# Sums of weight blocks in a gated recurrence: by VectorE from plain loads, and x's block sums kept out of the weight ring

## The chip, the cores and the metric

The kernel runs on one core of one Trainium2 chip. The metric is the device time of one execution in microseconds (us); of several runs the median is given. TensorE does the matrix products, VectorE and ScalarE the elementwise work, GpSimd (POOL) some products of the recurrence and every accumulating transfer, SyncE (SP) issues the plain loads.

## The reference

The program is a two-layer trunk on x of 512 frames by 1024 channels, all float32. Layer 0 is a gated linear recurrence (8 heads of 128 channels) and a squared-ReLU MLP; then one shared K/V is projected; layer 1 is differential attention over it and a second MLP. The change touches layer 0's mixer alone:

```python
proj = rms_norm(h) @ w_in
q, f, i, g = split(proj)            # queries, forget gates, values, output gates
k, log_f = gates(f)
o = hgrn2_recurrence(silu(q), k, log_f, i)
o = rms_norm(o) * silu(g)           # then @ w_out
```

## The kernel before, in words

Everything is held transposed (channels on partitions). Each float32 operand of a product is split into a rounded part ("hi") and a remainder ("lo"), and TensorE makes three matmuls for one: hi by hi, hi by lo, lo by hi. Weights arrive by SP into a ring of four raw slots (tag `raw`), are split by ScalarE (hi) and VectorE (lo) into rings of eight slots (tags `whi`, `wlo`), and free those when the last matmul that reads them is done. `split_b` (line 194) makes both parts by engines. `split_d` (line 184) lets ScalarE write hi and the negated hi, and an accumulating transfer of POOL's queue adds the weights from memory to the latter; it reads the raw slot only on ScalarE.

The mixer (`hgrn`, line 790) goes over four pairs of heads. For every head it projects q and f (`qf`), and spawns a chain (`head`, line 799) of gating, seven levels of a recursive scan, the state (`st`, lines 872 to 880), the output (`o`, lines 882 to 887) and a norm. The state's later chunks are made by VectorE at line 879, and the `o` products need them. The output gates of pairs 1 to 3 (`gates_pair`, line 902) and the values of pairs 2 and 3 (`values_pairs`, line 956) are made by a seven-product scheme: the weight matrix is cut in four blocks (0: A11, 1: A22, 2: A12, 3: A21), and four sums of blocks are wanted beside the blocks themselves: s1 = 3 + 1, s3 = 3 + 0, s2 = 0 + s1, s4 = 2 + s2. The products come in the order a11, s1, a12, s2, s4, s3, a22. Four sums of x's blocks meet them (`block_sums`, line 694): it runs as a chain, in the tiles `e` and `f` that are taken from the raw ring.

For a gates pair SP loads blocks 0 and 2 into `ra`, block 3 twice into the halves of `rs`, and block 1 into `rd`; POOL's queue then adds blocks 0 and 1 to `rs` by an accumulating transfer (line 910), which gives s3 and s1. VectorE makes s2 and s4 at lines 915 and 916. For the values every sum s1, s3 is likewise a load of block 3 (line 965) and an accumulating transfer on top (line 970).

The order on TensorE is written out by the program itself: `Plan` (line 45) steps through the chains by costs of its own (the `W_` constants) and the yields. On the other engines and queues a scheduler fixes the order when the kernel is built, by priority (chains are put ahead, `CHAIN_AHEAD`) and by its own reckoning of when each instruction could start. Every engine then runs its list in order: an instruction whose input is late holds up all behind it.

```python
            g.dma_start(rs, src[:, 0:2, :], accum_op=ALU.add)                       # 910
            v.tensor_tensor(ra[:, 0, :], ra[:, 0, :], rs[:, 1, :], op=ALU.add)      # 915
                v.scalar_tensor_tensor(st[:, c, :], st[:, c - 1, :], tcur[:, c:c + 1], ps[:, c * P:(c + 1) * P],   # 879
```

Of the kernel before, what the change touches and what calls it, by code (L numbers as in the profile page):

```python
# [9 lines left out]
F32 = mybir.dt.float32  # L10
F32R = mybir.dt.float32r
# [3 lines left out]
ALU = mybir.AluOpType  # L15
AX = mybir.AxisListType

P = 128
D = 1024
S = 512  # L20
# [68 lines left out]
def trunk_kernel(ctx: ExitStack, tc: tile.TileContext, x_t, w_qf, w_g, w_gs, w_i, w_is, w_ao, w_kv, w_q, w_bo, w_up, w_us, w_dn,  # L89
# [33 lines left out]
    xlo = [cp.tile([P, 2, S], F32R, name=f"xlo{i}") for i in range(4)]  # L123
    xraw = [cp.tile([P, 2, S], F32, tag=f"uhi{i}", name=f"xraw{i}", bufs=1) for i in range(4)]
    uhi = [cp.tile([P, 2, S], F32R, tag=f"uhi{i}", name=f"uhi{i}", bufs=1) for i in range(4)]
    ulo = [cp.tile([P, 2, S], F32R, name=f"ulo{i}") for i in range(4)]

    res = [x_t.rearrange("(k p) t -> p k t", p=P)[:, :, lo:hi] for lo, hi in ((0, 256), (256, 512))]
    gn = cp.tile([P, G_N], F32, name="gn")
# [564 lines left out]
    def block_sums(xs, ts):  # L694

        gain = gn[:, G_APRE:G_APRE + 8]
        e, f = [wp.tile([P, 4, 256], F32, tag="raw", name=f"sum_x{i}", bufs=4) for i in range(2)]

        def split(src, sign, n):
            if n < 3:  # L700
                hi, lo = [wp.tile([P, 4, 256], F32R, tag=t, name=f"{t}_x{n}", bufs=8) for t in ("whi", "wlo")]
            else:
                hi, lo = [u[3].rearrange("p j (r t) -> p (j r) t", r=2) for u in (uhi, ulo)]
            a.activation(hi, src, AF.Copy, scale=sign)
            if sign > 0:
                v.tensor_tensor(lo, src, hi.bitcast(F32), op=ALU.subtract)
            else:
                v.scalar_tensor_tensor(lo, src, -1.0, hi.bitcast(F32), op0=ALU.mult, op1=ALU.subtract)
            ts.append([(hi[:, r, :], lo[:, r, :]) for r in range(4)])

        def odd(n, out, op):

            for r in range(4):
                v.scalar_tensor_tensor(out[:, r], xs[2 * r + 1][:, n * 256:n * 256 + 256], gain[:, 2 * r + 1:2 * r + 2],
                                       out[:, r], op0=ALU.mult, op1=op)

        for r in range(4):
            for n, t in enumerate((e, f)):
                a.activation(t[:, r], xs[2 * r][:, n * 256:n * 256 + 256], AF.Copy, scale=gain[:, 2 * r:2 * r + 1])
        v.tensor_tensor(e, e, f, op=ALU.subtract)  # L720
        split(e, 1.0, 0)
        yield 8.0
        odd(1, f, ALU.subtract)
        split(f, 1.0, 1)
        yield 8.0
        odd(1, e, ALU.add)
        split(e, -1.0, 2)
        yield 8.0
        odd(0, e, ALU.subtract)
        split(e, -1.0, 3)  # L730

# [58 lines left out]
    def hgrn(hp, w0, xs):  # L790
# [108 lines left out]
        def banks(name):  # L899
            return [mmt(f"{name}_{n}") for n in "xyz"]  # L900

        def gates_pair(p):

            src, nm = w_gs[p - 1], f"gs{p}"
            ra = wp.tile([P, 2, 512], F32, tag="raw", name=f"raw_a{nm}", bufs=4)
            nc.sync.dma_start(ra, src[:, 0:3:2, :])
            rs = wp.tile([P, 2, 512], F32, tag="raw", name=f"raw_s{nm}", bufs=4)
            for i in range(2):
                nc.sync.dma_start(rs[:, i, :], src[:, 3, :])
            g.dma_start(rs, src[:, 0:2, :], accum_op=ALU.add)  # L910
            rd = wp.tile([P, 1, 512], F32, tag="raw", name=f"raw_d{nm}", bufs=4)
            nc.sync.dma_start(rd, src[:, 1:2, :])
            a11, a12 = split_d(ra, src[:, 0:3:2, :], f"a{nm}")
            s3, s1 = split_b(rs, f"s{nm}")
            v.tensor_tensor(ra[:, 0, :], ra[:, 0, :], rs[:, 1, :], op=ALU.add)
            v.tensor_tensor(ra[:, 1, :], ra[:, 1, :], ra[:, 0, :], op=ALU.add)
            s2, s4 = split_b(ra, f"t{nm}")
            a22, = split_d(rd, src[:, 1:2, :], f"d{nm}")
            x, y, z = [b[:, 0:256] for b in banks(nm)]
            g0, g1 = ggs[2 * p], ggs[2 * p + 1] = [hp.tile([P, S], F32, tag="g", name=f"g_{2 * p + j}", bufs=4) for j in range(2)]  # L920
            lo, hi = slice(0, 256), slice(256, 512)
            t1, t3, t2, t4 = ts

            def prod(ps, w, b, first):
                for k in range(4):
                    mm3(ps, w[0][:, k * P:(k + 1) * P], w[1][:, k * P:(k + 1) * P], *b[k], first and k == 0, k == 3, True)
                    yield 0

            def swish(gg, sign):
                if sign > 0:  # L930
                    v.tensor_tensor(gg, gg, rb, op=ALU.mult)
                else:
                    v.scalar_tensor_tensor(gg, gg, -1.0, rb, op0=ALU.mult, op1=ALU.mult)
                e = hp.tile([P, S], F32, tag="e", name=f"e{nm}{sign}", bufs=1)
                a.activation(e, gg, AF.Sigmoid)
                v.tensor_tensor(gg, gg, e, op=ALU.mult)

            yield from prod(x, a11, xpart(0, 0), True)
            a.activation(g0[:, lo], x, AF.Copy)
            yield from prod(z, s1, t1, True)  # L940
            a.activation(g1[:, hi], z, AF.Copy)
            yield from prod(y, a12, xpart(1, 0), True)
            v.tensor_tensor(g0[:, lo], y, g0[:, lo], op=ALU.add)
            yield from prod(x, s2, t2, False)
            a.activation(g0[:, hi], x, AF.Copy)
            yield from prod(z, s4, xpart(1, 1), False)
            v.tensor_tensor(g0[:, hi], z, g0[:, hi], op=ALU.add)
            swish(g0, 1)
            yield from prod(x, s3, t3, False)
            v.tensor_tensor(g1[:, hi], x, g1[:, hi], op=ALU.add)  # L950
            a.activation(g1[:, lo], x, AF.Copy)
            yield from prod(y, a22, t4, True)
            v.tensor_tensor(g1[:, lo], y, g1[:, lo], op=ALU.add)
            swish(g1, -1)

        def values_pairs():
# [6 lines left out]
            def block(n, i):  # L963
                r = raw(n)
                nc.sync.dma_start(r, w_is[:, i:i + 1, :])
                return r

            def summed(n, i):
                r = block(n, 3)
                g.dma_start(r, w_is[:, i:i + 1, :], accum_op=ALU.add)  # L970
                return r

            ra = block("a", 0)
            a11, = split_d(ra, w_is[:, 0:1, :], f"a11{nm}")
            rs = summed("s1", 1)
            s1, = split_b(rs, f"s1{nm}")
            rb_ = block("b", 2)
            a12, = split_d(rb_, w_is[:, 2:3, :], f"a12{nm}")
            v.tensor_tensor(ra, ra, rs, op=ALU.add)
            s2, = split_b(ra, f"s2{nm}")  # L980
            v.tensor_tensor(rb_, rb_, ra, op=ALU.add)
            s4, = split_b(rb_, f"s4{nm}")
            s3, = split_b(summed("s3", 0), f"s3{nm}")
            a22, = split_d(block("d", 1), w_is[:, 1:2, :], f"a22{nm}")
            x, y, z = [b.rearrange("p (m f) -> p m f", m=2) for b in banks(nm)]
            v0, v1 = vts[2], vts[3] = [hp.tile([P, 4, 256], F32, tag="vt", name=f"vt{p}", bufs=3) for p in (2, 3)]
            t1, t3, t2, t4 = ts
# [35 lines left out]
        for p in range(4):  # L1023
# [42 lines left out]
            else:  # L1066
# [2 lines left out]
                    yield until(("mix", 2 * p - 4), ("mix", 2 * p - 3))  # L1069
                if p == 2:  # L1070
                    yield from values_pairs()
                yield from gates_pair(p)
            done(("g", p))

    def values(ps, wv, t2):
# [276 lines left out]
```

## Time and profile before

| what | us |
|---|---|
| median of 3 runs | 1283.62 |
| lowest and highest of them | 1283.18, 1285.72 |
| the profiled execution, its own time | 1281.38 |
| its span, first to last instruction | 1279.3 |
| TensorE busy in the span | 1241.0 |
| VectorE, ScalarE, POOL busy | 820.6, 674.1, 100.2 |

The profile is one execution, separate from the three runs; its time lies 2.08 above its span and 2.24 below their median. The recurrence takes the first quarter of the span; TensorE's mean granted clock is 0.991 of full speed. A timeline row of the trace has the start, the duration, engine, line, operation with the tiles written and read, their shapes and the count; in brackets stands how long the engine was idle before it and what ended that. A transfer's row on SP, SPq or POOL is its issue; when it lands is told apart.

### The profile page before, as it was taken

What the parts mean: (1) busy time and instruction counts of PE and PEld (TensorE: products, weight loads), DVE (VectorE), ACT (ScalarE), POOL (GpSimd) and SP (SyncE); (2) the same over time, 40 slices, a digit from 0 to 9 for tenths busy, and PEclk for the clock granted to TensorE, in tenths of its full rate; (3) what the DMA queues carried; (4) which work ended last, traced back from release to release, by engine and by line L of the source; (5) the groups of instructions that cost most, each with busy time, mean ns of one, the idle gap of its engine ahead of it and who ended that gap; (6) DMA issues with size and microseconds to landing.
All of it is one profiled execution on the core that took longest, in us unless ns stands there. A gap on an engine that the chain in (4) does not pass through costs nothing.

```text
span 1279.3 us, 21468 instructions
## 1 busy us (share of the span) xinstructions
PE 1241.0 (97%) x8440; PEld 1125.2 (88%) x8440; DVE 820.6 (64%) x1646; ACT 674.1 (53%) x1248; POOL 100.2 (8%) x171
## 2 busy tenths in 40 slices
PE   9989997999999999999999999999999999999996
PEld 7778897899997988989999887889998898998996
DVE  7857783785863654745659977665785473653646
ACT  7435545435861652734645877665784271561732
POOL 0202211101000000000100000001000000000010
PEclk9999999999999999999999999999999999999999
DMA  7143848342547563564625523314236356363531
GB/s 240 57 101 102 170 108 193 79 137 90 173 130 134 138 176 91 166 148 104 201 73 168 149 66 100 112 38 132 79 122 180 98 168 142 103 194 70 157 108 66
DMA packets 58502, 161.94 MB, mean 127 GB/s; under 512 B 6529, under 2 KB 8834, under 8 KB 58402
## 3 DMA queue, kind: packets, MB, share of 16 engines
q1 hardware_dynamic: 46400, 121.13, 30.1%
q0 software_dynamic: 11760, 39.33, 14.8%
q8 instruction: 66, 1.08, 0.3%
q14 instruction: 34, 0.28, 0.1%
q10 hardware_dynamic: 242, 0.13, 0.1%
HBM read 150.86 MB, written 9.70 MB: 126 GB/s over the span
## 4 chain that ended last, share of the span: by engine, by line
PE 64%; DVE 5%; ACT 4%; DMA 3%; issue 2%; DVEq 0%; ACTq 0%; POOLq 0%; SPq 0%
PE dn L114 21%; PE ux L114 7%; PE up L114 7%; PE kq L114 6%; PE dn_h L114 5%; PE bo_h L114 3%; PE uz L114 3%; PE ao_h L114 3%; DMA raw_s<-in_w_us_dram 3%; PE v L114 2%; PE lg L114 2%; PE uy L114 1%; PE ao L114 1%; DVE wlo_s L200 1%; PE pt L119 1%
## 5 line engine op out<-in xcount | busy, mean ns | idle before, releaser
L114 PE MATMUL dn<-uhi,whi_dn 128*128 128x512 f32 x384 | 152.1, 396 | 0.0
L114 PE MATMUL dn<-ulo,whi_dn 128*128 128x512 f32 x384 | 152.0, 396 | 0.0
L114 PE MATMUL dn<-uhi,wlo_dn 128*128 128x512 f32 x384 | 151.9, 396 | 0.0
L114 PEld LDWEIGHTS dn<-uhi,whi_dn 128*128 128x128 f32 x384 | 72.3, 188 | 17.7 <-ACT r L562 0.7
L114 PEld LDWEIGHTS dn<-uhi,wlo_dn 128*128 128x128 f32 x384 | 72.3, 188 | 17.3
L114 PEld LDWEIGHTS dn<-ulo,whi_dn 128*128 128x128 f32 x384 | 72.3, 188 | 16.8
L199 ACT ACTIVATE whi_a<-raw_a 128x1024 fp32r<-128x1024 f32 x24 | 25.4, 1059 | 116.3 <-PE dn L114 113.1
L172 DVE TENSOR_TENSOR wlo_dn<-raw_dn,whi_dn 128x1024 fp32r<-128x1024 f32 x64 | 76.5, 1219 | 5.3 <-ACT whi_dn L171 4.6
L467 DVE TENSOR_TENSOR ulo<-r,uhi 128x1024 fp32r<-128x1024 f32 (+1 forms) x40 | 40.2, 1010 | 53.2 <-ACT uhi L466 53.1
L114 PE MATMUL up<-xhi,whi_up 128*128 128x256 f32 x256 | 72.1, 282 | 0.0
L114 PE MATMUL up<-xhi,wlo_up 128*128 128x256 f32 x256 | 71.6, 280 | 0.5 <-DVE wlo_up L172 0.5
L114 PE MATMUL up<-xlo,whi_up 128*128 128x256 f32 x256 | 71.4, 279 | 0.0
L171 ACT ACTIVATE whi_dn<-raw_dn 128x1024 fp32r<-128x1024 f32 x64 | 65.7, 1051 | 6.5 <-PE ux L114 2.9
L114 PE MATMUL dn_h<-uhi,whi_dn 128*128 128x256 f32 x240 | 66.7, 278 | 0.0
L114 PE MATMUL dn_h<-uhi,wlo_dn 128*128 128x256 f32 x240 | 66.3, 276 | 0.0
L114 PE MATMUL dn_h<-ulo,whi_dn 128*128 128x256 f32 x240 | 66.3, 276 | 0.0
L609 DVE TENSOR_TENSOR zacc<-dn,zacc 128x512 f32<-128x512 f32 x32 | 22.1, 690 | 59.1 <-PE dn L114 59.0
L511 POOL DMA_DIRECT2D raw_s<-in_w_us_dram x24 | 20.8, 865 | 487.2 <-DMA raw_s<-in_w_us_dram 335.2
L114 PE MATMUL qf<-xhi,whi_qf 128*128 128x512 f32 x128 | 53.0, 414 | 0.8 <-ACT xhi L678 0.8
L114 PE MATMUL qf<-xhi,wlo_qf 128*128 128x512 f32 x128 | 50.7, 396 | 1.4 <-DMA wlo_qf<-in_w_qf_dram 1.4
L199 ACT ACTIVATE whi_t<-raw_a 128x1024 fp32r<-128x1024 f32 x24 | 25.5, 1061 | 49.4 <-PE dn L114 27.2
L114 PE MATMUL qf<-xlo,whi_qf 128*128 128x512 f32 x128 | 50.9, 397 | 0.3 <-DVE xlo L679 0.3
(530 smaller groups left out, 4139.2 us busy)
## 6 DMA issues: line engine op xcount, KB each, us to landing
raw_dn<-in_w_dn_dram SPq DMA_DIRECT2D x64, 512.0 KB, 4.3
raw_a<-in_w_us_dram SPq DMA_DIRECT2D x24, 512.0 KB, 4.2
raw_s<-in_w_us_dram SPq DMA_DIRECT2D x48, 256.0 KB, 4.2
raw_s<-in_w_us_dram POOLq DMA_DIRECT2D x24, 512.0 KB, 6.4
raw_up<-in_w_up_dram SPq DMA_DIRECT2D x16, 512.0 KB, 3.9
raw_wkv<-in_w_kv_dram SPq DMA_DIRECT2D x16, 512.0 KB, 3.8
raw_qf<-in_w_qf_dram SPq DMA_DIRECT2D x14, 512.0 KB, 3.9
raw_d<-in_w_us_dram SPq DMA_DIRECT2D x12, 512.0 KB, 4.4
```

Of the source, the lines that this page charges most:

```text
L114: nc.tensor.matmul(out, lhsT, rhs, **kw)
L119: nc.tensor.transpose(out, in_, identity)
L171: last_split[:] = [a.activation(hi, raw, AF.Copy)]
L172: v.tensor_tensor(lo, raw, hi.bitcast(F32), op=ALU.subtract)
L199: a.activation(hi, raw, AF.Copy)
L200: v.tensor_tensor(lo, raw, hi.bitcast(F32), op=ALU.subtract)
L467: v.tensor_tensor(ulo[pr][:, :, lo:hi], r, uhi[pr][:, :, lo:hi].bitcast(F32), op=ALU.subtract)
L511: g.dma_start(rs, ws[p, :, 0:2, :], accum_op=ALU.add)
L609: v.tensor_tensor(z, pss[n4], z, op=ALU.add)
```

## The change

Three things are edited.

1. `block_sums` takes `e` and `f` from two new tiles that share memory with `ulo[1]` and `ulo[2]` (where the mixer's output goes later), so that the raw ring keeps four slots for weights. Its steps are spaced anew: a pause of 2 after each of the four pairs of ScalarE copies, then 5 in place of 8 between the sums.
2. A gates pair loads blocks 0 and 2 into `ra` and blocks 1 and 3 into `rs`, each once. `split_d` of block 1 comes before the sums; then VectorE adds block 3 to block 1 (s1) and block 0 to block 3 (s3) in place. The accumulating transfer of line 910, the second load of block 3 and the tile `rd` are gone. The weights' part becomes a function of its own, called at the same point.
3. The values load blocks 0, 3, 1, 3 and 2, and VectorE makes s1 and s3; the two accumulating transfers of line 970 are gone. Block 2 is now the fifth of the five tiles that go through the ring of four.

```diff
--- before.py
+++ after.py
@@ -123,7 +123,8 @@
     xlo = [cp.tile([P, 2, S], F32R, name=f"xlo{i}") for i in range(4)]
     xraw = [cp.tile([P, 2, S], F32, tag=f"uhi{i}", name=f"xraw{i}", bufs=1) for i in range(4)]
     uhi = [cp.tile([P, 2, S], F32R, tag=f"uhi{i}", name=f"uhi{i}", bufs=1) for i in range(4)]
-    ulo = [cp.tile([P, 2, S], F32R, name=f"ulo{i}") for i in range(4)]
+    sums = [cp.tile([P, 4, 256], F32, tag=f"ulo{i}", name=f"sums{i}", bufs=1) for i in (1, 2)]
+    ulo = [cp.tile([P, 2, S], F32R, tag=f"ulo{i}", name=f"ulo{i}", bufs=1) for i in range(4)]
 
     res = [x_t.rearrange("(k p) t -> p k t", p=P)[:, :, lo:hi] for lo, hi in ((0, 256), (256, 512))]
     gn = cp.tile([P, G_N], F32, name="gn")
@@ -694,7 +695,7 @@
     def block_sums(xs, ts):
 
         gain = gn[:, G_APRE:G_APRE + 8]
-        e, f = [wp.tile([P, 4, 256], F32, tag="raw", name=f"sum_x{i}", bufs=4) for i in range(2)]
+        e, f = sums
 
         def split(src, sign, n):
             if n < 3:
@@ -717,15 +718,16 @@
         for r in range(4):
             for n, t in enumerate((e, f)):
                 a.activation(t[:, r], xs[2 * r][:, n * 256:n * 256 + 256], AF.Copy, scale=gain[:, 2 * r:2 * r + 1])
+            yield 2.0
         v.tensor_tensor(e, e, f, op=ALU.subtract)
         split(e, 1.0, 0)
-        yield 8.0
+        yield 5.0
         odd(1, f, ALU.subtract)
         split(f, 1.0, 1)
-        yield 8.0
+        yield 5.0
         odd(1, e, ALU.add)
         split(e, -1.0, 2)
-        yield 8.0
+        yield 5.0
         odd(0, e, ALU.subtract)
         split(e, -1.0, 3)
 
@@ -899,23 +901,26 @@
         def banks(name):
             return [mmt(f"{name}_{n}") for n in "xyz"]
 
-        def gates_pair(p):
+        def gate_weights(p):
 
             src, nm = w_gs[p - 1], f"gs{p}"
-            ra = wp.tile([P, 2, 512], F32, tag="raw", name=f"raw_a{nm}", bufs=4)
+            ra, rs = [wp.tile([P, 2, 512], F32, tag="raw", name=f"raw_{n}{nm}", bufs=4) for n in "as"]
             nc.sync.dma_start(ra, src[:, 0:3:2, :])
-            rs = wp.tile([P, 2, 512], F32, tag="raw", name=f"raw_s{nm}", bufs=4)
-            for i in range(2):
-                nc.sync.dma_start(rs[:, i, :], src[:, 3, :])
-            g.dma_start(rs, src[:, 0:2, :], accum_op=ALU.add)
-            rd = wp.tile([P, 1, 512], F32, tag="raw", name=f"raw_d{nm}", bufs=4)
-            nc.sync.dma_start(rd, src[:, 1:2, :])
+            nc.sync.dma_start(rs, src[:, 1:4:2, :])
             a11, a12 = split_d(ra, src[:, 0:3:2, :], f"a{nm}")
-            s3, s1 = split_b(rs, f"s{nm}")
-            v.tensor_tensor(ra[:, 0, :], ra[:, 0, :], rs[:, 1, :], op=ALU.add)
+            a22, = split_d(rs[:, 0:1, :], src[:, 1:2, :], f"d{nm}")
+            v.tensor_tensor(rs[:, 0, :], rs[:, 0, :], rs[:, 1, :], op=ALU.add)
+            v.tensor_tensor(rs[:, 1, :], rs[:, 1, :], ra[:, 0, :], op=ALU.add)
+            s1, s3 = split_b(rs, f"s{nm}")
+            v.tensor_tensor(ra[:, 0, :], ra[:, 0, :], rs[:, 0, :], op=ALU.add)
             v.tensor_tensor(ra[:, 1, :], ra[:, 1, :], ra[:, 0, :], op=ALU.add)
             s2, s4 = split_b(ra, f"t{nm}")
-            a22, = split_d(rd, src[:, 1:2, :], f"d{nm}")
+            return a11, a12, a22, s1, s2, s3, s4
+
+        def gates_pair(p, ws):
+
+            nm = f"gs{p}"
+            a11, a12, a22, s1, s2, s3, s4 = ws
             x, y, z = [b[:, 0:256] for b in banks(nm)]
             g0, g1 = ggs[2 * p], ggs[2 * p + 1] = [hp.tile([P, S], F32, tag="g", name=f"g_{2 * p + j}", bufs=4) for j in range(2)]
             lo, hi = slice(0, 256), slice(256, 512)
@@ -965,23 +970,20 @@
                 nc.sync.dma_start(r, w_is[:, i:i + 1, :])
                 return r
 
-            def summed(n, i):
-                r = block(n, 3)
-                g.dma_start(r, w_is[:, i:i + 1, :], accum_op=ALU.add)
-                return r
-
-            ra = block("a", 0)
+            ra, rs, rt = block("a", 0), block("s", 3), block("d", 1)
             a11, = split_d(ra, w_is[:, 0:1, :], f"a11{nm}")
-            rs = summed("s1", 1)
+            v.tensor_tensor(rs, rs, rt, op=ALU.add)
             s1, = split_b(rs, f"s1{nm}")
+            r3 = block("t", 3)
+            v.tensor_tensor(r3, r3, ra, op=ALU.add)
+            v.tensor_tensor(ra, ra, rs, op=ALU.add)
             rb_ = block("b", 2)
             a12, = split_d(rb_, w_is[:, 2:3, :], f"a12{nm}")
-            v.tensor_tensor(ra, ra, rs, op=ALU.add)
             s2, = split_b(ra, f"s2{nm}")
             v.tensor_tensor(rb_, rb_, ra, op=ALU.add)
             s4, = split_b(rb_, f"s4{nm}")
-            s3, = split_b(summed("s3", 0), f"s3{nm}")
-            a22, = split_d(block("d", 1), w_is[:, 1:2, :], f"a22{nm}")
+            s3, = split_b(r3, f"s3{nm}")
+            a22, = split_d(rt, w_is[:, 1:2, :], f"a22{nm}")
             x, y, z = [b.rearrange("p (m f) -> p m f", m=2) for b in banks(nm)]
             v0, v1 = vts[2], vts[3] = [hp.tile([P, 4, 256], F32, tag="vt", name=f"vt{p}", bufs=3) for p in (2, 3)]
             t1, t3, t2, t4 = ts
@@ -1069,7 +1071,7 @@
                     yield until(("mix", 2 * p - 4), ("mix", 2 * p - 3))
                 if p == 2:
                     yield from values_pairs()
-                yield from gates_pair(p)
+                yield from gates_pair(p, gate_weights(p))
             done(("g", p))
 
     def values(ps, wv, t2):
```

## Rows read from the trace of the kernel before

**Rows 1.** The page: busy time of each engine, share of the span, instructions.

```profile
PE 1241.0 (97%) x8440; PEld 1125.2 (88%) x8440; DVE 820.6 (64%) x1646; ACT 674.1 (53%) x1248; POOL 100.2 (8%) x171
```

**Rows 2.** Waits of TensorE, 0 to 300 us: total us, times, longest us.

```profile
PE o L114 <- DVE st L879: 11.5, 3, 6.3
PE g L114 <- ACT qc L812: 1.8, 2, 1.3
...
PE qf L114 <- DMA wlo_qf<-in_w_qf_dram: 1.4, 1, 1.4
```

**Rows 3.** Timeline of TensorE: the `o` products that waited for the state.

```profile
92.54 0.80 PE L114 MATMUL o<-st,q 128*128 128x128 f32 x2 [4.84 <-DVE st L879]
...
156.69 0.49 PE L114 MATMUL o<-st,q 128*128 128x128 f32 x2 [0.38 <-DVE st L879]
...
224.41 0.80 PE L114 MATMUL o<-st,q 128*128 128x128 f32 x2 [6.33 <-DVE st L879]
```

**Rows 4.** Timeline of VectorE around the two long waits.

```profile
82.01 0.69 DVE L795 TENSOR_TENSOR g<-g,rb 128x512 f32<-128x512 f32 x1 [0.71 <-PE g L114]
90.33 0.69 DVE L915 TENSOR_TENSOR raw_ags<-raw_ags,raw_sgs 128x512 f32<-128x512 f32 x1 [7.63 <-DMA raw_sgs<-in_w_gs_dram]
...
92.14 1.12 DVE L879 SCALAR_TENSOR_TENSOR st<-st,tt,st 128x128 f32<-128x128 f32 x4
...
223.41 0.69 DVE L915 TENSOR_TENSOR raw_ags<-raw_ags,raw_sgs 128x512 f32<-128x512 f32 x1 [9.58 <-DMA raw_sgs<-in_w_gs_dram]
224.01 1.12 DVE L879 SCALAR_TENSOR_TENSOR st<-st,tt,st 128x128 f32<-128x128 f32 x4
```

**Rows 5.** Issues by SP and POOL for these sums; last, landing of line 910's transfers.

```profile
77.01 0.82 SPq L909 DMA_DIRECT2D raw_sgs<-in_w_gs_dram  x2
...
82.77 1.04 POOL L910 DMA_DIRECT2D raw_sgs<-in_w_gs_dram  x1 [32.49 <-DVE g L795]
...
216.07 0.85 POOL L910 DMA_DIRECT2D raw_sgs<-in_w_gs_dram  x1 [5.02 <-DMA raw_sgs<-in_w_gs_dram]
...
DMA to landing us min/median/max: 6.7/7.3/7.5
```

**Rows 6.** Windows after the two waits: length, busy by engine, PEclk, DMA share, GB/s.

```profile
92.50:96.30 3.80, 3.76 (x21) 3.77 (x21) 1.52 (x8) 1.14 (x8) 0.00 (x0) 0.59 0.01 2
...
224.40:229.00 4.60, 4.59 (x21) 4.58 (x22) 2.79 (x13) 1.15 (x9) 0.00 (x0) 0.53 0.66 122
```

**Rows 7.** Timeline of ScalarE: parts of pair 1's gate weights.

```profile
81.77 1.06 ACT L190 ACTIVATE whi_ags<-raw_ags 128x1024 fp32r<-128x1024 f32 x1 [1.74 <-PE g L114]
...
101.20 1.06 ACT L199 ACTIVATE whi_sgs<-raw_sgs 128x1024 fp32r<-128x1024 f32 x1 [0.31 <-PE qf L114]
...
104.08 1.05 ACT L199 ACTIVATE whi_tgs<-raw_ags 128x1024 fp32r<-128x1024 f32 x1
...
113.27 0.63 ACT L190 ACTIVATE whi_dgs<-raw_dgs 128x512 fp32r<-128x512 f32 x1 [0.43 <-PE qf L114]
```

**Rows 8.** Timeline of TensorE: first matmul of pair 1's fourth gates product (s2).

```profile
123.39 0.28 PE L114 MATMUL gs_x<-whi_x,whi_tgs 128*128 128x256 f32 x1
```

**Rows 9.** Values: a load's issue, landing of line 965's loads, VectorE, TensorE.

```profile
135.17 0.33 SPq L965 DMA_DIRECT2D raw_s3is<-in_w_is_dram  x1
...
DMA to landing us min/median/max: 3.6/4.2/9.4
...
139.08 1.22 DVE L979 TENSOR_TENSOR raw_ais<-raw_ais,raw_s1is 128x1024 f32<-128x1024 f32 x1
...
141.20 0.35 DVE L879 SCALAR_TENSOR_TENSOR st<-st,tt,st 128x128 f32<-128x128 f32 x1 [0.20 <-ACT st L877]
...
142.98 0.39 PE L114 MATMUL o<-st,q 128*128 128x128 f32 x2
```

**Rows 10.** Timeline of VectorE: a block sum's split among the first gates' work.

```profile
46.25 1.31 DVE L706 TENSOR_TENSOR wlo_x<-sum_x,whi_x 128x1024 fp32r<-128x1024 f32 x1
```

**Rows 11.** Landing of line 191's accumulating transfers, 60 to 260 us.

```profile
DMA to landing us min/median/max: 4.8/8.7/11.2
```

## The prediction

> **What bounds the kernel now.** The page comes first: TensorE is busy for 97% of the span and VectorE for 64% [rows 1], so time is won where TensorE stands still, or where it runs at a lower clock. The waits of TensorE in the first 300 us say where that is: 11.5 us are `o` products that wait for line 879 of VectorE, 1.8 are `g` products behind ScalarE's line 812, and 1.4 are a `qf` product behind an accumulating transfer [rows 2]. The timeline of TensorE puts nearly all of the first sum into two places, 4.84 us up to 92.54 and 6.33 us up to 224.41; the third is 0.38 [rows 3].
>
> Line 879 is not slow: its four pieces take 1.12 us. VectorE's timeline shows what stands ahead of them: line 915, the sum of s1 into block 0, for which VectorE stood idle 7.63 us and 9.58 us until the tile `raw_sgs` had come [rows 4]. So the chain of the first stall is this. SP could issue the loads of block 3 only at 77.01; POOL's accumulating transfer on top of them was issued at 82.77, the one of pair 3 at 216.07 after a wait of 5.02 for those loads; and such a transfer lands 6.7 to 7.5 us after its issue [rows 5]. 82.77 + 7.5 = 90.3 and 216.07 + 7.3 = 223.4, where line 915 starts in both cases. The reader should see that nobody needed line 915 then: TensorE came to the fourth gates product, its consumer, at 123.39 [rows 8]. The sum blocks only because VectorE runs its list in order.
>
> The wait costs more than its length. In the window behind each of them the granted clock is 0.59 and 0.53 of full speed with TensorE busy throughout [rows 6], that is mostly its lower level of 1.2 GHz after it had stood.
>
> **The change, part by part.** All sums are made against the profiled execution, 1281.38 us (span 1279.3 and 2.08 around it).
>
> *The first stall.* The accumulating transfer goes; s1 and s3 are VectorE sums of plainly loaded blocks. They cannot block line 879 in the same way, for this reason: the new sum overwrites block 1, so it waits until ScalarE has read block 1 in `split_d`, and that needs a slot of the part rings. In the kernel before, the first part of pair 1 took a slot at 81.77 and the next one came only at 101.20, when `qf` matmuls had freed it [rows 7]; those matmuls stand behind the stalled `o` products in TensorE's order. An order in which VectorE waits for the new sum ahead of line 879 would be a circle, so the sum comes behind. Gain: 4.84 of waiting, and in the window behind it 3.80 x (1 - 0.59) = 1.56 of clock. What is late next is line 879 itself; the third wait on it is 0.38 [rows 3], which I take as what is left, between 0 and 0.8. So 4.84 + 1.56 - 0.4 = 6.0.
>
> *The second stall*, pair 3, by the same reasoning: 6.33 + 4.60 x (1 - 0.53) = 6.33 + 2.16 = 8.49, less 0.4: 8.1.
>
> *The `qf` wait* of 1.37 (1.4 in [rows 2]) hangs on an accumulating transfer of line 191, which lands between 4.8 and 11.2 us after issue, 8.7 in the middle [rows 11]. This transfer stays, but the pair's accumulating transfer and 768 KB of traffic around it go. At 4.8 the wait vanishes, at 11.2 it grows by some 2 us. I take half of it as gained, 0.7; ends -2 and +1.4.
>
> *The two `g` waits*, 1.8 together [rows 2], stand in the stretch where VectorE makes x's block sums amid the first heads' gating: the split at 46.25 takes 1.31 us there [rows 10], as much as the longer wait. The pauses put these sums later in priority, and the new tiles let them begin earlier; either moves work out of this stretch, but not surely. Ends: +1.8, and -1.3 if one more split of that size falls into it. I take half, 0.9. Their results are met first in the gates products of pair 1, the fourth of which starts at 123.39 [rows 8], over 70 us later, so that lateness of the sums itself costs nothing.
>
> *What is added.* Two VectorE sums per gates pair of 0.69 us (the shape of line 915, [rows 4]) and two for the values of 1.22 (line 979, [rows 9]): 6 x 0.69 + 2 x 1.22 = 6.6 us. They are spread over some 150 us in which VectorE has idle time (36% over the whole span [rows 1]; the 7.63 and 9.58 us of [rows 4] come free besides) and nobody waits for them at once, so I cost them at nothing; without that cover they would cost at most 6.6.
>
> *What leaves the queues.* POOL: three transfers of line 910 and two of line 970, with the waits ahead of them (one of 5.02 us, in which `split_d` transfers queued behind it [rows 5]). SP: per gates pair four loads become two; values keep five. In bytes 3 x 768 KB + 1 MB less. Nothing but the `qf` wait above feels it on TensorE, so nothing more is booked.
>
> *The order of the parts.* Block 1's parts are now made second, not last, so those of s1/s3 and of s2/s4 get their slots one release later: by the old times 104.08 in place of 101.20, and 113.27 in place of 104.08 [rows 7]. From 113.27, with 1.06 on ScalarE and 1.22 on VectorE, s2 is there by 116; it is used at 123.39 [rows 8]. Cost nothing; the cover is 7 us. In the values the fifth load (block 2) waits for a slot as the fifth did before, so equal.
>
> After the recurrence the same instructions run in the same order on TensorE; nothing.
>
> Sum: 6.0 + 8.1 + 0.7 + 0.9 = 15.7, so 1281.38 - 15.7 = 1265.7 for the profiled execution. The median of the runs lies 2.24 above that execution, and I give the time for the median: 1267.9, rounded 1268.
>
> **The rivals.**
>
> *A new wait at the values.* Here the sum of blocks 3 and 1 and that of 3 and 0 wait for nothing but their loads, so the scheduler may put them where it thinks the data has come, ahead of a line 879, and this is the old fault with a plain load in place of an accumulating one. For it: the load at 135.17 is the last of four, and line 965's loads land between 3.6 and 9.4 us after issue [rows 9]. At 9.4 the last is there at 144.6, its sum is done at 145.8, and line 879, which ran at 141.20, ends at 146.2; the `o` products used it from 142.98 [rows 9], so TensorE would wait some 3.2 us and lose up to 1.6 of clock: 4.8. Against it: at 3.6 the load is there at 138.8, ahead of line 979, and nothing waits. The likely price lies between: 3.5, so 1271.5, and at most 1272.8. The Trainium skill, DMA: Bandwidth & Descriptors, section "Issuing engines are not separate DMA queues", has all transfers, whoever issues them, share the same 16 engines and interleave. By that rule taking out the accumulating transfers of line 970 brings these loads toward the short end and the price of this rival toward 0, while the `split_d` transfers that stay keep it from getting there.
>
> *Only one of the stalls goes.* If the block sums' new place or pauses leave a part slot free early, the argument from the circle fails for one pair, and a sum may again stand ahead of line 879, now behind a plain load or behind ScalarE. Then 6.0 or 8.1 is lost from the gain: 1274 to 1276. Against it: the rings have the same slots and the same users as before.
>
> *Slower.* The new gates sums stand behind ScalarE's `split_d`, which stands behind a slot that TensorE frees. If the scheduler reckons that slot freed too early, it lists the sums ahead of the levels of another head's scan, which then wait with VectorE while TensorE runs dry. Each us of misjudgment costs a us of VectorE at each of the four places (three pairs, the values). It decides from 4 us at each place, 16 in all, which eats the 15.7; at 5 us each the time would be 1268 + 20 = 1288. Against it: in the kernel before ScalarE's parts waited in the same manner for slots, and the idle time ahead of them was 0.31 to 1.74 us [rows 7].
>
> **How the numbers follow.** The forecast, both stalls gone and nothing new over 1 us: 0.62, 1268. The wait at the values: 0.20, 1269.5 to 1273. Only one stall gone: 0.10, 1274 to 1276. A mix that ends within 0.2% of before (2.6 us, about what a measurement of this kernel can tell): 0.03. Slower: 0.05. The low end is the forecast with all of the uncertain gains: 0.7 + 0.9 more from the `qf` and `g` waits, 0.8 from what I left on line 879, and some 1.5 for the distance between executions: 1264 and a little less, 1263. The high end takes in the case of one stall: 1276. So 0.92 for faster, 0.03 for same, 0.05 for slower.
>
> **What the profile after would show.** Right: no idle VectorE ahead of the gates' sums; no `o` wait over 1 us; a clock of 1.00 through the recurrence; no accumulating transfer into `raw_s` of gates or values; the MLPs as before but some 15 us earlier. Wrong, if line 879 again follows a VectorE wait on a transfer (first rival: at the values, around 130 to 140 us), if `gs` or `is` products wait for VectorE's parts, or if the `g` waits have grown.

## The result, and the profile after

The changed kernel takes 1273.28 us (median of four executions, 1272.13 to 1273.89); the kernel before, four times beside it, 1284.17. The ratio is 0.9913, with a 95% interval of 0.9896 to 0.993. That is 10.9 us gained where 15.7 were forecast: the time lies in the range, 5.3 above the number. The profiled execution took 1273.18 us, its span 1271.4, with a mean clock of 0.994.

TensorE issues the same 8440 matmuls in the same order as before, so the start of each can be compared in the two traces. Of the kernel after, the line of busy times, and the waits of TensorE in the first 300 us (total, times, longest):

```profile
PE 1240.0 (98%) x8440; PEld 1122.8 (88%) x8440; DVE 825.8 (65%) x1654; ACT 673.9 (53%) x1248; POOL 95.6 (8%) x166
```

```profile
PE ps_sp L114 <- DVE dg L755: 3.0, 1, 3.0
PE qf L114 <- DMA wlo_qf<-in_w_qf_dram: 1.7, 1, 1.7
PE ao_h L114 <- ACT uhi L643: 1.4, 1, 1.4
PE qf L114 <- ACT xhi L679: 1.4, 1, 1.4
```

Against [rows 2], the 11.5 us of `o` and the 1.8 of `g` are gone, the `qf` wait stays, and a new one stands at the top: `ps_sp`, a product that TensorE makes near 40 us (it spreads the norm's factors of x over the partitions), behind line 755 of VectorE. VectorE's timeline shows why the `o` waits went. The lines of `st` (881, formerly 879) and the first sum of each gates pair (912):

```profile
90.94 1.47 DVE L881 SCALAR_TENSOR_TENSOR st<-st,tt,st 128x128 f32<-128x128 f32 x4 [0.76 <-ACT st L879]
...
101.70 0.69 DVE L912 TENSOR_TENSOR raw_sgs<-raw_sgs 128x512 f32<-128x512 f32 x1 [0.17 <-ACT wlo_dgs L190]
...
214.04 0.35 DVE L881 SCALAR_TENSOR_TENSOR st<-st,tt,st 128x128 f32<-128x128 f32 x1 [2.74 <-ACT st L879]
...
224.79 0.69 DVE L912 TENSOR_TENSOR raw_sgs<-raw_sgs 128x512 f32<-128x512 f32 x1 [0.17 <-ACT wlo_dgs L190]
```

In both pairs the sum now comes some 10 us behind the state, and what released it is `wlo_dgs`, ScalarE's part of block 1: the order that the prediction deduced. In [rows 4] it came ahead. TensorE's windows, in the columns of [rows 6], give the clock back at the first stall, and show where it was lost instead:

```profile
40.10:44.50 4.40, 4.39 (x10) 2.87 (x11) 2.25 (x4) 0.83 (x2) 0.00 (x0) 0.62 0.16 63
92.60:96.30 3.70, 3.70 (x29) 3.46 (x28) 1.31 (x8) 2.29 (x16) 0.00 (x0) 1.00 0.61 112
```

**The new wait.** First VectorE's timeline of the kernel after ahead of that product, then TensorE's:

```profile
34.21 1.22 DVE L707 TENSOR_TENSOR wlo_x<-sums,whi_x 128x1024 fp32r<-128x1024 f32 x1
...
35.89 1.23 DVE L173 TENSOR_TENSOR wlo_qf<-raw_qf,whi_qf 128x1024 fp32r<-128x1024 f32 x1 [0.39 <-ACT whi_qf L172]
...
37.10 0.48 DVE L715 SCALAR_TENSOR_TENSOR sums<-xraw,gn,sums 128x256 f32<-128x256 f32 x1
37.50 0.15 DVE L252 TENSOR_TENSOR nt<-nt,nx 128x4 f32<-128x4 f32 x1
37.57 0.48 DVE L715 SCALAR_TENSOR_TENSOR sums<-xraw,gn,sums 128x256 f32<-128x256 f32 x1
...
39.37 0.68 DVE L755 TENSOR_TENSOR dg<-ident,rcol 128x512 f32<-128x512 f32 x1
```

```profile
36.67 0.40 PE L114 MATMUL i<-whi_wi,xlo 128*128 128x512 f32 x1
40.11 2.07 PE L114 MATMUL ps_sp<-dg,ones 128*128 128x512 f32 x2 [3.04 <-DVE dg L755]
```

`dg` is what the norm of x leads to, and the norm's short steps (lines 251 to 253, 0.16 us each) alternate with the sums of x's blocks (line 715, 0.48 each, four of them) behind a split of the first sum (line 707). In the kernel before the same `dg` was there some 7 us earlier, and its block sum came after it. Of these 7 us, 2.55 are the later start; the norm's steps up to `dg` then took 4.1 longer. By an estimate from the rows some 2.2 of that are block sums and their split, and 1.9 are one more split of weights (line 173, at 35.89) and idle time ahead of this and another. Here VectorE and TensorE of the kernel before:

```profile
32.76 0.68 DVE L753 TENSOR_TENSOR dg<-ident,rcol 128x512 f32<-128x512 f32 x1
33.36 1.22 DVE L720 TENSOR_TENSOR sum_x<-sum_x,sum_x 128x1024 f32<-128x1024 f32 x1
```

```profile
34.36 1.02 PE L114 MATMUL ps_sp<-dg,ones 128*128 128x512 f32 x2
```

What brought the sums forward is on ScalarE. In the kernel before the copies of x's blocks (line 719 there, 720 after) waited until weights had left the raw ring; in the kernel after they need only x:

```profile
28.82 0.91 ACT L719 ACTIVATE sum_x<-xraw,gn 128x256 f32<-128x256 f32 x2 [0.46 <-DVE wlo_wi L172]
30.03 2.51 ACT L719 ACTIVATE sum_x<-xraw,gn 128x256 f32<-128x256 f32 x6 [0.30 <-DVE wlo_wi L172]
```

```profile
4.26 0.89 ACT L720 ACTIVATE sums<-xraw,gn 128x256 f32<-128x256 f32 x2
5.05 0.71 ACT L679 ACTIVATE xhi<-xraw,gn 128x512 fp32r<-128x512 f32 x1
...
9.60 0.91 ACT L720 ACTIVATE sums<-xraw,gn 128x256 f32<-128x256 f32 x2 [0.75 <-DMA xraw<-in_x_t_dram]
```

**Where the time stands.** Start of the same matmul, after less before (us, by the starts in the two traces; negative is earlier):

| time of before | what has passed | difference | step |
|---|---|---|---|
| 30 | start: x's parts 0.93 late, then clock | +2.55 | +2.55 |
| 44 | `ps_sp` wait 3.04 and 1.85 behind it, most of it clock | +7.44 | +4.89 |
| 56 | both `g` waits gone | +5.15 | -2.29 |
| 97 | first `o` stall and its clock | -1.41 | -6.56 |
| 158 | third `o` wait and what stood beside it | -2.47 | -1.06 |
| 216.7 | `qf` waits of pair 3 | -2.03 | +0.44 |
| 229 | second stall and its clock | -10.78 | -8.75 |
| 292 | end of the mixer | -10.96 | -0.18 |
| 1268 | end | -8.28 | +2.68 |

So the two traces differ by 10.96 at the end of the mixer, and 2.68 are lost again in the MLPs and the second layer, whose code is the same. The medians differ by 10.9; before's profiled execution lies 2.8 below the median of its four, after's 0.1 below its own. That last step is therefore put down to the two executions, not to the change: over the same stretch, with the same code, the other ten kernels moved between 1.8 earlier and 2.3 later, so 2.68 is only a little beyond them. No run takes it apart.

### The profile page after: what moved, and what is told of

It is laid out like the page before. It is cut to its first block, busy times and chain, and to the rows that moved or that the text cites. A ratio compares the mean times of both kernels' runs of the same rounds, so it can differ in the third digit from the quotient of the medians.

```text
span 1271.4 us, 21443 instructions
## 1 busy us (share of the span) xinstructions
PE 1240.0 (98%) x8440; PEld 1122.8 (88%) x8440; DVE 825.8 (65%) x1654; ACT 673.9 (53%) x1248; POOL 95.6 (8%) x166
## 4 chain that ended last, share of the span: by engine, by line
PE 79%; issue 6%; DMA 6%; DVE 5%; ACT 4%; POOL 0%; SPq 0%; DVEq 0%; ACTq 0%; POOLq 0%
PE dn L114 20%; PE qf L114 7%; PE up L114 7%; PE ux L114 6%; PE kq L114 6%; PE ao_h L114 3%; DMA raw_s<-in_w_us_dram 3%; PE bo_h L114 3%; PE dn_h L114 3%; PE uz L114 3%; PE gl L114 3%; PE v L114 3%; PE g L114 2%; PE lg L114 2%; PE i L114 2%
## 5 line engine op out<-in xcount | busy, mean ns | idle before, releaser
L114 PEld LDWEIGHTS dn<-uhi,wlo_dn 128*128 128x128 f32 x384 | 72.2, 188 | 17.3
```

The source lines that it names most:

```text
L114: nc.tensor.matmul(out, lhsT, rhs, **kw)
```

## The experiments

Two things were to be settled: what the shortfall of 5 us is, and whether the accumulating transfers were the fault at all or only the place of the sums in VectorE's list. In the edits `tc.issue_after(x)` puts an instruction behind x in the order of issue and changes nothing else. Times are medians; the ratio with its interval is against the kernel before in the same session (1284.17 for the kernel after, 1282.8 to 1282.9 for the others), so kernels are compared by it. The intervals of seven, e1, e2, e4, e5, e8, e10 and e11, overlap, so their medians do not rank them; what each edit moved is read from the traces. In the last column `qf` is the wait for a transfer in pair 3, `gl` a product of a head's scan levels.

| kernel | us | ratio, 95% | largest among the waits spoken of |
|---|---|---|---|
| after | 1273.28 | 0.9913, 0.9896 to 0.993 | `ps_sp` 3.0, `qf` 1.7 |
| e1_ring | 1266.92 | 0.9879, 0.9859 to 0.9899 | `qf` 1.8, `gl` 0.7 |
| e2_hold | 1267.89 | 0.9873, 0.9854 to 0.9893 | `qf` 1.7, `ps_sp` 0.8 |
| e3_blocks_only | 1280.32 | 0.9985, 0.9972 to 0.9999 | `o` 6.4, `ps_sp` 3.0 |
| e4_sums_only | 1267.52 | 0.988, 0.9865 to 0.9895 | `qf` 1.8, `gl` 1.5, `g` 1.3 |
| e5_order_only | 1267.57 | 0.9882, 0.9867 to 0.9898 | `qf` 1.3, `g` 1.3 |
| e7_old_spacing | 1273.27 | 0.9931, 0.9909 to 0.9953 | `ps_sp` 3.0, `qf` 1.7 |
| e8_hold_both | 1265.3 | 0.9875, 0.9856 to 0.9895 | `qf` 1.8, `g` 0.6 |
| e9_d_last | 1273.2 | 0.9933, 0.9915 to 0.995 | `o` 6.2 |
| e10_behind_st | 1264.51 | 0.9859, 0.9841 to 0.9878 | `gl` 0.7, `g` 0.6 |
| e11_accum_held | 1266.15 | 0.9877, 0.9855 to 0.9899 | `gl` 0.9, `qf` 0.6 |

The same comparison of TensorE's starts with the kernel before, one execution each, at seven times of the kernel before. 30 to 40 holds `ps_sp`, 60 to 100 the first stall, 200 to 229 the second:

| kernel | 30 | 40 | 60 | 100 | 200 | 229 | 300 |
|---|---|---|---|---|---|---|---|
| after | 2.6 | 7.4 | 5.2 | -1.4 | -2.5 | -10.8 | -11.1 |
| e1_ring | 0.3 | 0.3 | -0.8 | -7.3 | -7.6 | -15.9 | -16.2 |
| e2_hold | 0.0 | 1.0 | -0.9 | -7.4 | -8.5 | -16.8 | -17.1 |
| e3_blocks_only | 2.8 | 6.1 | 3.8 | -2.8 | -2.8 | -2.7 | -2.9 |
| e4_sums_only | 2.1 | 2.1 | 2.1 | -4.5 | -4.0 | -12.2 | -12.6 |
| e5_order_only | 0.1 | 0.1 | 0.2 | -6.4 | -6.4 | -15.1 | -15.0 |
| e7_old_spacing | 2.6 | 8.8 | 6.7 | 0.1 | -0.7 | -9.0 | -9.4 |
| e8_hold_both | 0.0 | 0.0 | -1.5 | -8.1 | -9.0 | -17.3 | -17.6 |
| e9_d_last | 0.1 | 0.1 | -1.4 | -8.0 | -8.5 | -10.4 | -10.4 |
| e10_behind_st | 0.2 | 0.2 | -1.2 | -7.8 | -8.1 | -17.7 | -18.1 |
| e11_accum_held | 0.2 | 0.2 | -1.2 | -7.8 | -7.8 | -17.1 | -16.1 |

**e2_hold**: the kernel after, with ScalarE's eight copies held behind the last split of the values' first weights.

```diff
-                a.activation(t[:, r], xs[2 * r][:, n * 256:n * 256 + 256], AF.Copy, ...)
+                with tc.issue_after(behind.ins):
+                    a.activation(t[:, r], xs[2 * r][:, n * 256:n * 256 + 256], AF.Copy, ...)
```

> The changed kernel, with ScalarE's eight copies of x's blocks kept behind the last split of the first values' weights. Theory (early copies: out of the ring the copies may start as soon as x is there, go ahead of x's own parts and of the sums of squares, and cost 2.5 us at the start and 4.9 us before the product ps_sp): these 7.3 us come back, less up to 2.1 us if the two g waits return, so 1266 to 1268.5, with no ps_sp wait over 0.5 us. Rival (the late start comes from the fuller load queue or from the new sums, not from the copies): 1272 to 1274, with the ps_sp wait of 3 us still there.

1267.89 us (1262.81 to 1268.42), a ratio of 0.9873, whose interval lies wholly below that of the kernel after. The start is level with the kernel before, and of the `ps_sp` wait 0.8 is left, because VectorE's sums still stand ahead of `dg`. Holding the eight copies gives back the shortfall: -17.1 at 300 us where the kernel after has -11.1.

**e3_blocks_only**: the kernel before with edit 1 alone (the tiles out of the ring and the new spacing).

> The kernel before with the first edit alone: x's block sums out of the ring and spaced anew, gates and values still summed by accumulating transfers. Theory (early copies cost some 5 us net at the start; the freed ring slots let the first pair's loads and its accumulating transfer come early, so that the first o wait of 4.8 us goes with its 1.6 us of clock, while the second of 6.3 us stays): 1284.2 + 5.2 - 6.4 = 1283, between 1281.5 and 1284.5, with a ps_sp wait near 3 us and an o wait near 6 us. Rival (copies cost nothing): 1277 to 1278.

1280.32 (1277.12 to 1284.45 in ten executions), 1.2 below the expected range, which was counted from 1284.2 where the kernel before beside it took 1282.82. The same 3.0 us `ps_sp` wait stands there without any change to the weights, so edit 1 makes it. And edit 1 alone takes away the first stall, as this run's expectation had it and the prediction had not. VectorE's timeline of this kernel:

```profile
87.60 0.69 DVE L917 TENSOR_TENSOR raw_ags<-raw_ags,raw_sgs 128x512 f32<-128x512 f32 x1 [1.11 <-ACT wlo_ags L190]
...
89.57 1.47 DVE L881 SCALAR_TENSOR_TENSOR st<-st,tt,st 128x128 f32<-128x128 f32 x4
...
220.55 0.69 DVE L917 TENSOR_TENSOR raw_ags<-raw_ags,raw_sgs 128x512 f32<-128x512 f32 x1 [9.51 <-DMA raw_sgs<-in_w_gs_dram]
221.16 1.12 DVE L881 SCALAR_TENSOR_TENSOR st<-st,tt,st 128x128 f32<-128x128 f32 x4
```

The sum (line 917) still stands ahead of the state, but in pair 1 its transfer was done in time: SP issued the loads of block 3 at 65.81 and POOL the transfer at 71.03, against 77.01 and 82.77 in [rows 5]. Pair 3 is as in [rows 4].

**e4_sums_only**: the kernel after with x's block sums as in the kernel before (ring and old spacing).

> The changed kernel with x's block sums wholly as before (in the ring, spaced as before); gates and values summed by VectorE. Theory (the new sums wait for a part slot and so fall behind line 879 whatever the ring holds): both long o waits gone with their clock, 1284.2 - 14.5 = 1269.7, between 1268 and 1271.5, the g waits of 1.8 us still there. Rival (the first wait goes only because the ring is free, so that it comes back here): 1275 to 1277, with an o wait of 3 us or more near 90 us.

1267.52 (1265.92 to 1269.52): both stalls gone, the `g` waits of 1.8 back, no `ps_sp` wait; 0.5 below the expected range. Edits 2 and 3 alone beat the whole change (0.988 against 0.9913, intervals apart).

**e5_order_only**: the kernel before, all transfers as they were, with the two VectorE sums of a gates pair held behind the last state line.

```diff
-            v.tensor_tensor(ra[:, 0, :], ra[:, 0, :], rs[:, 1, :], op=ALU.add)
-            v.tensor_tensor(ra[:, 1, :], ra[:, 1, :], ra[:, 0, :], op=ALU.add)
+            with tc.issue_after(last_st[0].ins):
+                v.tensor_tensor(ra[:, 0, :], ra[:, 0, :], rs[:, 1, :], op=ALU.add)
+                v.tensor_tensor(ra[:, 1, :], ra[:, 1, :], ra[:, 0, :], op=ALU.add)
```

> The kernel before, all transfers as they were, with the two VectorE sums of a gates pair (lines 915 and 916) kept behind the state's line 879 of the heads before. Theory (order: VectorE's list was the fault and the accumulating transfer's 7 us harmless): both long o waits go, 1284.2 - 14.5 = 1269.7, between 1268 and 1272. Rival (traffic: the accumulating transfers hold up the loads and what hangs on them, so that the wait moves elsewhere): 1278 or more.

1267.57 (1265.9 to 1270.67): the whole gain of e4 without touching a transfer. VectorE's timeline:

```profile
85.95 1.47 DVE L879 SCALAR_TENSOR_TENSOR st<-st,tt,st 128x128 f32<-128x128 f32 x4 [0.76 <-ACT st L877]
88.70 0.69 DVE L916 TENSOR_TENSOR raw_ags<-raw_ags,raw_sgs 128x512 f32<-128x512 f32 x1 [1.28 <-DMA raw_sgs<-in_w_gs_dram]
```

The sum still waits for its accumulating transfer, but behind the state, where nobody stands in line. The order was the fault.

**e1_ring**: the kernel after with x's sums back in the ring, the new spacing kept. **e7_old_spacing**: the opposite, out of the ring with the old spacing.

```diff
-        e, f = sums
+        e, f = [wp.tile([P, 4, 256], F32, tag="raw", name=f"sum_x{i}", bufs=4) for i in range(2)]
```

```diff
-            yield 2.0
-        yield 5.0
+        yield 8.0
```

> The changed kernel with x's block sums back in tiles of the weight ring, their new spacing kept. Theory (the free tiles are what lets copies and sums start too early; the spacing is harmless): like the kernel with block sums wholly as before, 1266 to 1269, no ps_sp wait over 0.5 us. Rival (the spacing is at fault): 1271 to 1274 with a ps_sp wait of 2 to 3 us.

> The changed kernel with x's block sums out of the ring as changed, but with the old spacing (no pause between copies, 8 between sums). Theory (free tiles): 1271.5 to 1274.5, the ps_sp wait of 2.5 to 3.5 us still there. Rival (spacing): 1266 to 1269 without that wait.

e1 takes 1266.92 (1264.78 to 1268.45) and has no `ps_sp` wait; its `g` wait is 0.5 against 1.8 in e4, so the spacing does help there. e7 takes 1273.27 (1270.94 to 1273.61) with the wait of 3.0. Their intervals do not meet. The free tiles cost some 5 us (at 300 us, -16.2 in e1 against -11.1 in the kernel after), whatever the spacing.

**e8_hold_both**: e2, and VectorE's first block sum held behind `dg`.

```diff
-        v.tensor_tensor(e, e, f, op=ALU.subtract)
+        with tc.issue_after(dg_made[0].ins):
+            v.tensor_tensor(e, e, f, op=ALU.subtract)
```

> The kernel with the copies held (e2), and VectorE's first block sum also kept behind the tile dg that ps_sp reads. Theory (what is left of the ps_sp wait, 0.8 us, is block sums among the small steps of the norm): that wait goes and some clock with it, 1266 to 1267.5 where e2 had 1267.9. Rival (other work fills the same place): 1267.5 to 1269, wait still 0.5 us or more.

1265.3 (1264.39 to 1268.46), no `ps_sp` wait; its time cannot be told from that of e2. ScalarE and VectorE of this kernel:

```profile
25.64 3.29 ACT L722 ACTIVATE sums<-xraw,gn 128x256 f32<-128x256 f32 x8
```

```profile
31.70 0.69 DVE L758 TENSOR_TENSOR dg<-ident,rcol 128x512 f32<-128x512 f32 x1
32.30 1.22 DVE L725 TENSOR_TENSOR sums<-sums,sums 128x1024 f32<-128x1024 f32 x1
```

The copies run as one batch at 25.64, `dg` comes at 31.70 as early as in the kernel before, and the tiles outside the ring then do no harm.

**e9_d_last**: e8 with block 1 loaded a second time into a tile of its own (`rd`) and its parts made last, as in the kernel before. The sum then waits for no part slot, only for plain loads.

```diff
+            nc.sync.dma_start(rd, src[:, 1:2, :])
-            a22, = split_d(rs[:, 0:1, :], src[:, 1:2, :], f"d{nm}")
 ...
+            a22, = split_d(rd, src[:, 1:2, :], f"d{nm}")
```

> The kernel e8 with block 1 of a gates pair loaded a second time into a slot of its own, so that its parts come last again and the sums s1 and s3 wait for nothing but their loads. Theory A (parts one slot later are what keeps the qf wait of 1.7 us): that wait falls under 0.5 us, 1264.5 to 1266.5. Theory B (only the wait for a part slot keeps the sums behind line 879; the load of pair 3 took 11 us in the changed kernel): an o wait of 1 to 5 us comes back near 210 us, 1268 to 1273.

1273.2 (1271.31 to 1275.71). The second stall is back, longer than the 1 to 5 us expected, though the sum's blocks come by plain loads alone. VectorE, TensorE, and the issue with its size and time to landing in the stretch from 190 us:

```profile
209.54 0.69 DVE L916 TENSOR_TENSOR raw_sgs<-raw_sgs 128x512 f32<-128x512 f32 x1 [8.27 <-DMA raw_sgs<-in_w_gs_dram]
...
214.68 1.11 DVE L884 SCALAR_TENSOR_TENSOR st<-st,tt,st 128x128 f32<-128x128 f32 x4
```

```profile
214.26 0.80 PE L114 MATMUL o<-st,q 128*128 128x128 f32 x2 [6.21 <-ACT st L882]
```

```profile
raw_sgs<-in_w_gs_dram SPq DMA_DIRECT2D x1, 512.0 KB, 10.9
```

The profile names ScalarE's line 882, the first state piece, as the releaser; that came at 213.95, behind line 945 on ScalarE, which had waited 7.47 for VectorE. So ahead of it is again the sum, before which VectorE stood idle for 8.27 until a plain load came. Pair 1 shows no stall: there the sum ran at 78.17 without waiting. In exchange the `qf` wait falls to 0.3.

**e10_behind_st**: e9, with the first sum held behind the last state line, as in e5.

> The kernel e9 (block 1 loaded apart, its parts last) with the first VectorE sum of each gates pair kept behind the state's line of the heads before. Theory (the list's order alone makes the o wait; nothing needs the sum early): the 6.2 us o wait goes with its clock, the qf wait stays under 0.5 us, 1273.2 - 6.2 - 2 = 1265, less 1 to 2 us against e8, so 1262.5 to 1265.5. Rival (the late loads of pair 3 hold up something else once line 879 is free): 1267 or more.

1264.51 (1263.17 to 1265.88), ratio 0.9859: no `o` wait and a `qf` wait of 0.4. VectorE in pair 3:

```profile
207.11 1.12 DVE L884 SCALAR_TENSOR_TENSOR st<-st,tt,st 128x128 f32<-128x128 f32 x4 [1.36 <-ACT st L882]
...
209.77 0.69 DVE L917 TENSOR_TENSOR raw_sgs<-raw_sgs 128x512 f32<-128x512 f32 x1 [1.53 <-DMA raw_sgs<-in_w_gs_dram]
```

It has the lowest median of all, 18.4 below the kernel before beside it, where the kernel after stood 10.9 below its own; against the six others named above the overlap leaves that open. e9 and e10 differ by this one edge alone.

**e11_accum_held**: the kernel before, with the accumulating transfers of gates and values, but with x's block sums as in e8, and VectorE's two sums of a gates pair held as in e5.

> Gates and values summed by POOL's accumulating transfers as in the kernel before, lines 915 and 916 kept behind line 879 (as in e5), and x's block sums out of the ring but held on both engines as in e8. Theory (the accumulating transfers are harmless once the order is right): within 2 us of e8 and e10, 1263 to 1267. Rival (their 3.3 MB and their place in POOL's queue cost several us beside the plain loads): 1269 or more, with new waits on transfers.

1266.15 (1265.14 to 1267.96), interval 0.9855 to 0.9899 against 0.9841 to 0.9878 of e10: they overlap. With the sums in the right place, what plain loads are worth cannot be told from nothing.

## Why the prediction was right, and which step failed

**The two stalls: right.** Forecast 6.0 and 8.1 with their clock, measured 6.56 and 8.75. The 0.4 left over for line 879 in each was too careful (the `o` products waited for nothing). The third `o` wait, 0.38 in [rows 3], went with them; that stretch gave 1.06 where nothing was booked. One sign that the prediction named did not come: the clock was not 1.00 through the recurrence (0.62 behind `ps_sp`).

**The argument from the circle: right, and it carries all of pair 3.** In pair 1 either part of the change is enough: the stall goes with edit 1 alone (e3) and without it (e4). The sum came behind the state because it waited for ScalarE's part of block 1, which needs a slot of the part ring (ScalarE makes it at 101.04 without idle time before it, so the slot shows in the order of the lists and not as a wait). e9 takes that one wait away, keeps the plain loads, and in pair 3 the stall is back with 6.21. So the gain does not come from "VectorE in place of an accumulating transfer"; e5 gets it with those transfers in place. The prediction named the fault (the list runs in order, and the sum is needed far later), and its second rival, a sum again ahead of the state behind a plain load, is exactly e9; it didn't happen in the kernel after.

**The step that failed: the two `g` waits, "I take half, 0.9", with ends +1.8 and -1.3.** The `g` waits did go (2.29). But the edit they were booked for cost 2.55 in the first 30 us and 4.89 at `ps_sp`: a gain of -5.15 with the 2.29 counted, 3.9 below the worse end. That the time lies in the range all the same is luck: its high end of 1276 was set for one stall left over, which did not happen. The prediction looked only at the stretch of the `g` waits and wrote that the new tiles "let them begin earlier". It did not follow that to its end: what the ring's slots had been holding back, and who else on ScalarE and VectorE had been served first because of it. The rows to read were ScalarE's copies at 28.82 and 30.03 of the kernel before, released by `wlo_wi`, and `dg` at 32.76 on VectorE, close ahead of TensorE's 34.36. The `ps_sp` part is shown by e1, e2, e7 and e8.

For the first 2.55 the runs are less plain: with free copies the start is 2.6, 2.8 and 2.6 late (after, e3, e7), and 0.0 to 0.3 in seven of the eight others, but 2.1 in e4, whose copies wait for the ring as before. The traces take it apart. In the kernel after, copies at 9.60 on ScalarE stand ahead of the next part of x, which comes at 10.41 in place of 9.47; TensorE waits 1.38 for it in place of 0.82 and is 0.93 late. The rest is clock, granted at 0.50 from 13 to 16 us (1.00 in the kernel before). In e4 the same part comes 0.53 late behind loads, TensorE waits 1.21, and the clock over these 3 us is 0.50 too. In e3 the wait there was 1.63 and the clock stayed at 1.00; its lateness is waits alone. So the copies bring the waits, but some 1.5 us of the 2.55 are clock, which e4 lost without them; why it fell in some executions and not in others stays open.

**The `qf` wait, "I take half of it as gained, 0.7", and "the order of the parts: cost nothing": wrong by 1.1, inside the ends of -2 and +1.4, and the two are one.** The wait of [rows 2] did go, and another took its place: net +0.44. Block 1's parts come second now, so ScalarE makes the parts of s2 and s4 of pair 2 later. The split of s2 and s4 and POOL's first `qf` transfer of pair 3, kernel before:

```profile
192.70 1.06 ACT L199 ACTIVATE whi_tgs<-raw_ags 128x1024 fp32r<-128x1024 f32 x1 [1.91 <-PE is_z L114]
```

```profile
201.08 0.85 POOL L191 DMA_DIRECT2D wlo_qf<-in_w_qf_dram  x1 [3.06 <-ACT sc L860]
```

and the kernel after, with the matmul that waited:

```profile
197.42 1.06 ACT L200 ACTIVATE whi_tgs<-raw_ags 128x1024 fp32r<-128x1024 f32 x1 [1.83 <-PE is_y L114]
```

```profile
201.21 0.86 POOL L192 DMA_DIRECT2D wlo_qf<-in_w_qf_dram  x1 [12.14 <-ACT wlo_qf L190]
```

```profile
210.43 0.50 PE L114 MATMUL qf<-xhi,wlo_qf 128*128 128x512 f32 x1 [1.73 <-DMA wlo_qf<-in_w_qf_dram]
```

TensorE is 2.48 earlier there, the transfer is not, because ScalarE made its part only at 199.86, behind that split; it lands 9.2 us after its issue, and TensorE meets it. The prediction had checked that s2 itself would be in time (7 us of cover) and left out what is queued behind that split on ScalarE. Over all kernels, block 1's parts second means a `qf` wait of 1.7 to 1.8 (after, e1, e2, e4, e7, e8), last means 0.3 to 1.4 (before, e3, e5, e9, e10, e11); e8 and e9, 1.8 against 0.3, differ only in this and in the second load of block 1 that it needs.

**The added sums and the emptier queues, booked at nothing: right** as far as the runs go; VectorE rose by 5.2 us of busy time (6.6 estimated for the sums), with no wait of TensorE behind line 912 to 916.

**The rival at the values** got its cause and not its effect. In the kernel after, VectorE did wait there for a plain load:

```profile
139.83 0.34 DVE L881 SCALAR_TENSOR_TENSOR st<-st,tt,st 128x128 f32<-128x128 f32 x1
140.69 0.34 DVE L881 SCALAR_TENSOR_TENSOR st<-st,tt,st 128x128 f32<-128x128 f32 x1
142.49 1.23 DVE L978 TENSOR_TENSOR raw_tis<-raw_tis,raw_ais 128x1024 f32<-128x1024 f32 x1 [1.46 <-DMA raw_tis<-in_w_is_dram]
```

but behind the state, so that 1.46 us cost TensorE nothing. The slower rival had no trace: no VectorE wait behind a part slot held up a scan.

By terms: 6.0, 8.1, 0.7 and 0.9 forecast, 15.7; 6.56, 8.75, -0.44, -5.15 and 1.06 found, 10.8. e1, the same change with x's sums left in the ring, stands 16.2 below the kernel before at 300 us of it, near the 15.7 of the forecast: the change without the part that failed.

## What to carry to other kernels

When an engine stands idle in front of an instruction that nobody needs yet, first try to put that instruction behind the one that is needed; only the order has to change, and another way of bringing the data can leave the fault in place (e5 against e9). A buffer taken out of a shared ring also takes away a wait that may have kept side work out of the way: look at what the freed work will run among, and hold it with an explicit edge to the last thing that must go first (e2, e8). When a part of the work is moved up in an engine's list, cost what is queued behind it and not only the part itself.

## What the runs showed of the hardware that was not expected

A single wait of 3.04 us at 40 us cost another 1.67 of clock, 4.40 x (1 - 0.62): TensorE, at 1.00 in the kernel before over these products, was granted 0.62 of 2.4 GHz in the 4.40 us after it, that is for most of it the lower level of 1.2 GHz. In the kernel before, the window is:

```profile
34.00:38.40 4.40, 4.40 (x19) 3.28 (x18) 4.40 (x6) 1.06 (x1) 0.00 (x0) 1.00 0.37 119
```

So a wait of 3 us was dearer by more than half.

The same plain load of 512 KB took 4.0 us to land in pair 1 of the kernel after and 11.0 in pair 3, where it was issued at 204.64 and others stood beside it: POOL issued accumulating transfers at 204.91, 207.66, 209.40 and 211.81, and SP a load at 200.93 and two from 207.39. Which of them held it up no run takes apart. From the rows of issues, 60 to 100 us and 190 to 216 us:

```profile
raw_sgs<-in_w_gs_dram SPq DMA_DIRECT2D x1, 512.0 KB, 4.0
```

```profile
raw_sgs<-in_w_gs_dram SPq DMA_DIRECT2D x1, 512.0 KB, 11.0
```

The long landing is half of why e9 stalls in pair 3 and not in pair 1. In pair 3 of e9 the load was issued at 198.60, only 2.7 us before VectorE was free for the sum (201.27), and took 10.9; by an estimate from the 4.0 of pair 1 it would have been there at 202.6, a wait of 1.3 in place of 8.27. In pair 1 it was issued at 62.05, 16 us before its sum. The rule cited in the prediction from the Trainium skill, DMA: Bandwidth & Descriptors, section "Issuing engines are not separate DMA queues" (transfers of all engines share the same 16 and interleave), agrees with this pair of rows, 4.0 against 11.0; the prediction drew on it only for the values, and the slow landing was dear in pair 3 of e9.
